# The instructions of a hybrid attention / DeltaNet layer, put in order by a scheduler with a timeline model instead of a plain one

## The chip, the cores and the metric

The kernel runs on one core of a Trainium2 chip. The metric is the device time of one execution in microseconds (us); lower is better. Before the change it is 937.15 us, the median of three runs (936.86 to 937.77).

The engines are named as in the profile: PE is the matrix engine (PEld its weight loads), DVE the vector engine, ACT the scalar engine, POOL the general-purpose engine, SP the engine that only issues transfers here. Each engine takes its instructions strictly in the order in which they stand in its own list. Semaphores tie the lists together.

## The reference

One layer of a diffusion backbone over 512 latent tokens and 256 context tokens, all in float32. The core of it is:

```python
mod = silu(c) @ w_ada + b_ada                       # adaLN, 6 vectors; mod_c the same from c_ctx
h  = rms_norm(x, g_norm1)   * (1 + sc1)  + sh1
hc = rms_norm(ctx, g_norm1) * (1 + csc1) + csh1
aq, ak, av, dq, dk, dv, dz, da, db, ga, gd = split_cols(h @ w_in)   # the same for hc
y_attn = window_ctx_attention(rope(q), rope(k), v, k_ctx, v_ctx, sink)      # 8 heads, 2 KV heads, window 128
_, s_cf, s_cb = bidir_delta(context inputs, zero state)              # gated DeltaNet, chunks of 64, two directions
o_dl, _, _    = bidir_delta(latent inputs, s_cf, s_cb)
y_d = rms_norm(o_dl) * silu(dz)
y = sigmoid(ga) * (y_attn @ w_br_attn) + sigmoid(gd) * (y_d @ w_br_dn)
x = x + gt1 * (y @ w_out)
x = x + gt2 * (square(relu(modulated_norm(x) @ w_mlp1)) @ w_mlp2)
```

The DeltaNet part inverts a unit-triangular 64 x 64 matrix for each chunk and head, and carries a 64 x 64 state per head through 4 context and 8 latent chunks, forwards and backwards.

## The kernel before, in words

Activations lie with channels on the 128 partitions and the 512 (or 256) tokens along the free axis. A float32 product is made of three matmuls on values split into a high and a low part (`mm3`: high x high, high x low, low x high; lines L289, L290, L291; the gate tiles do the same at L943, the attention branch at L988). Each weight tile of 128 x 1024 arrives by `wload`: a transfer by SP into one of four raw buffers, then a copy of the high part by ACT (L240) and a subtraction for the low part by DVE (L241):

```python
raw = sb.tile([P, KT, P], F32, tag="wr", bufs=NWR, name=nm("wr"))[:, :n]     # NWR = 4
nc.sync.dma_start(out=raw, in_=src)
A.activation(r32(hi), raw, AF.Copy)
V.tensor_tensor(r32(lo), raw, hi, op=ALU.subtract)
```

All other buffers in SBUF and PSUM come from an arena at fixed addresses, handed out in program order.

The program runs through these stages. In *startup* the adaLN vectors are made from `w_ada` (L207, L226) and the inputs are normalised and split. The *input projection* follows; meanwhile the DeltaNet's small 32 x 32 and 64 x 64 products are made (half products L699, decay sums L718), and the triangular matrices are inverted on DVE. The *attention* runs over 8 units of query block and KV head. Then come the 4 *context steps* of the DeltaNet's chain, with the branch projection (L988) and gate tiles (L943) woven in. The two *combines* put the inverted halves together: 64 matmuls of 32 x 32 at L793/L794, a copy by ACT, and 64 more at L803/L804, each of them two passes on PE. The 8 *latent steps* of the chain run PE L1055 -> DVE L1059, L1060 -> PE L1067 -> DVE L1073 -> PE L1086 (and L1104 for the output) -> DVE L1097 -> PE L1055 of the next step, for both directions in turn. Between these parts the program text puts gate-tile matmuls as fill (`FILL[3] = (8, 7, 3)` in each step) and one late adaLN column (`late_mod`: one 512 KB transfer into a raw weight buffer and one DVE multiply-and-sum at L1009):

```python
for n, _ in enumerate(steps(range(NCC, NC_))):
    run_fill(FILL[3][n % 3])
    if n % 3:
        run_late(LATE)
```

Then the chain's output is normalised and transposed (L1219, L1224, L1229), the DeltaNet branch and the output projection follow, the second norm (L1297 sums squares over partitions, once for each half of the tokens), and the MLP, some 330 us of `mm3` in a row.

The program text is only a first order. The whole program stands inside one `tile.TileContext`, and its scheduler makes each engine's list: it takes the instructions whose inputs are due by its own model of the time that each takes, and so moves them ahead of or behind one another, within the dependencies. The order around the change is therefore set by that model.

## Time and profile before

| | |
|---|---|
| median of three runs | 937.15 us (936.86 to 937.77) |
| the profiled execution | 938.35 us, its span 936.5 us |
| mean granted clock of PE | 0.991 |
| PE busy | 901.0 us, 96% of the span, 7736 matmuls |
| DVE busy | 596.2 us, 64% |
| ACT busy | 443.0 us, 47% |
| moved by DMA | 98.72 MB, 105 GB/s on average |

PE counts as busy also while its pipeline fills, so a busy PE is not one at its peak. The shares are averages over stages that differ a great deal: DVE is nearly full between 100 and 200 us and idle for more than half of the MLP.

### The profile page before, as it was taken

What the parts mean: (1) busy time and instruction counts of PE and PEld (TensorE: products, weight loads), DVE (VectorE), ACT (ScalarE), POOL (GpSimd) and SP (SyncE); (2) the same over time, 40 slices, a digit from 0 to 9 for tenths busy, and PEclk for the clock granted to TensorE, in tenths of its full rate; (3) what the DMA queues carried; (4) which work ended last, traced back from release to release, by engine and by line L of the source; (5) the groups of instructions that cost most, each with busy time, mean ns of one, the idle gap of its engine ahead of it and who ended that gap; (6) DMA issues with size and microseconds to landing.
All of it is one profiled execution on the core that took longest, in us unless ns stands there. A gap on an engine that the chain in (4) does not pass through costs nothing.

```text
span 936.5 us, 18158 instructions
## 1 busy us (share of the span) xinstructions
PE 901.0 (96%) x7736; PEld 730.0 (78%) x7736; DVE 596.2 (64%) x1013; ACT 443.0 (47%) x815; POOL 12.1 (1%) x26
## 2 busy tenths in 40 slices
PE   7999889999999999989999998999999999999998
PEld 5688667877777677778888888988888888888886
DVE  4666779997877998358875977982454235434411
ACT  5467635338567887475555434660243125213400
POOL 0000000000000001000000000000000000000000
PEclk8999989999999999999999999999999999999999
DMA  9921111210000132225424474481344124222111
GB/s 350 347 69 46 47 47 46 68 46 24 23 11 24 34 114 92 93 92 162 157 86 136 157 273 137 143 291 39 115 152 138 45 68 156 92 67 91 45 43 47
DMA packets 29600, 98.72 MB, mean 105 GB/s; under 512 B 3664, under 2 KB 4176, under 8 KB 29520
## 3 DMA queue, kind: packets, MB, share of 16 engines
q1 hardware_dynamic: 29520, 97.57, 31.5%
q8 instruction: 60, 0.98, 0.4%
q14 instruction: 20, 0.16, 0.1%
HBM read 95.46 MB, written 2.10 MB: 104 GB/s over the span
## 4 chain that ended last, share of the span: by engine, by line
PE 72%; DVE 12%; ACT 8%; DMA 4%; issue 3%; SPq 0%; DVEq 0%; ACTq 0%
PE banks L289 16%; PE banks L290 15%; PE banks L291 15%; PE banks L943 9%; PE banks L988 2%; DMA wr<-in_wm 2%; PE banks L1055 2%; DMA wa<-in_wada 2%; DVE wl L241 1%; ACT m L146 1%; PE banks L1086 1%; PE banks L1067 1%; PE banks L526 1%; DVE m L183 1%; PE banks L207 1%
## 5 line engine op out<-in xcount | busy, mean ns | idle before, releaser
L289 PE MATMUL banks<-m,m 128*128 128x512 f32 (+1 forms) x584 | 219.4, 379 | 3.4 <-ACT m L240 3.0
L290 PE MATMUL banks<-m,m 128*128 128x512 f32 (+1 forms) x584 | 219.0, 377 | 0.1
L291 PE MATMUL banks<-m,m 128*128 128x512 f32 (+1 forms) x584 | 218.9, 377 | 0.0
L240 ACT ACTIVATE m<-wr 128x1024 fp32r<-128x1024 f32 x67 | 70.8, 1058 | 157.9 <-PE banks L290 78.9
L289 PEld LDWEIGHTS banks<-m,m 128*128 128x128 f32 x584 | 109.2, 188 | 26.4 <-ACT m L240 3.1
L241 DVE TENSOR_TENSOR m<-wr,m 128x1024 fp32r<-128x1024 f32 x67 | 81.9, 1224 | 70.3 <-PE banks L290 34.2
L290 PEld LDWEIGHTS banks<-m,m 128*128 128x128 f32 x584 | 109.5, 188 | 21.7 <-DVE m L241 0.8
L291 PEld LDWEIGHTS banks<-m,m 128*128 128x128 f32 x584 | 109.3, 188 | 21.2 <-issue 0.8
L289 PE MATMUL banks<-m,wh 128*128 128x512 f32 (+1 forms) x312 | 114.1, 366 | 0.9 <-DVE m L1270 0.6
L291 PE MATMUL banks<-m,wl 128*128 128x512 f32 (+1 forms) x312 | 111.5, 360 | 2.3 <-DVE wl L241 2.3
L290 PE MATMUL banks<-m,wh 128*128 128x512 f32 (+1 forms) x312 | 111.0, 356 | 0.0
L943 PE MATMUL banks<-m,wh 128*128 128x512 f32 x320 | 103.9, 399 | 0.0
L1371 DVE SCALAR_TENSOR_TENSOR m<-banks,modT,m 128x512 f32<-128x512 f32 x32 | 24.0, 750 | 101.0 <-PE banks L291 101.0
L241 DVE TENSOR_TENSOR wl<-wr,wh 128x1024 fp32r<-128x1024 f32 (+1 forms) x60 | 64.7, 1079 | 28.4 <-ACT wh L240 28.2
L240 ACT ACTIVATE wh<-wr 128x1024 fp32r<-128x1024 f32 (+1 forms) x60 | 56.6, 944 | 31.5 <-PE banks L290 15.0
L943 PEld LDWEIGHTS banks<-m,wh 128*128 128x128 f32 x320 | 59.1, 188 | 12.1
L291 PEld LDWEIGHTS banks<-m,wl 128*128 128x128 f32 x312 | 58.8, 189 | 11.3 <-DVE wl L241 3.0
L289 PEld LDWEIGHTS banks<-m,wh 128*128 128x128 f32 x312 | 59.3, 190 | 10.4 <-DVE m L1270 0.8
L290 PEld LDWEIGHTS banks<-m,wh 128*128 128x128 f32 x312 | 59.3, 190 | 7.5 <-issue 0.2
L943 PE MATMUL banks<-m,wl 128*128 128x512 f32 x160 | 65.0, 406 | 0.0
L182 ACT ACTIVATE m<-m 128x512 fp32r<-128x512 f32 (+1 forms) x56 | 35.2, 631 | 48.9 <-DVE m L1354 21.1
L183 DVE TENSOR_TENSOR m<-m,m 128x512 fp32r<-128x512 f32 (+1 forms) x56 | 38.3, 689 | 18.8 <-ACT m L182 18.3
(231 smaller groups left out, 1274.7 us busy)
## 6 DMA issues: line engine op xcount, KB each, us to landing
wr<-in_wm SPq DMA_DIRECT2D x64, 512.0 KB, 3.5
wr<-in_win SPq DMA_DIRECT2D x39, 512.0 KB, 3.5
wa<-in_wada SPq DMA_DIRECT2D x32, 512.0 KB, 4.0
m<-in_wada SPq DMA_DIRECT2D x16, 512.0 KB, 10.2
m<-in_xT SPq DMA_DIRECT2D x8, 512.0 KB, 6.1
wr<-in_wbr SPq DMA_DIRECT2D x16, 256.0 KB, 2.7
wr<-in_wout SPq DMA_DIRECT2D x8, 512.0 KB, 4.7
out<-m SPq DMA_DIRECT2D x8, 256.0 KB, 2.0
```

What stands on the lines that cost most here:

```text
L146: r = A.activation(out_, in_, func, **kw)
L182: A.activation(r32(hi), src, AF.Copy)
L183: (eng or V).tensor_tensor(r32(lo), src, hi, op=ALU.subtract)
L240: A.activation(r32(hi), raw, AF.Copy)
L241: V.tensor_tensor(r32(lo), raw, hi, op=ALU.subtract)
L289: PE.matmul(acc, w[0][:, k, :], xhi, start=(start and i == 0), stop=False)
L290: PE.matmul(acc, w[0][:, k, :], xlo, start=False, stop=False)
L291: PE.matmul(acc, w[1][:, k, :], xhi, start=False, stop=(stop and i == n - 1))
L943: PE.matmul(acc.ap, w[x][:, k, :], hx[k][y], start=(k == p == 0), stop=(k == KT - 1 and p == 2))
L988: PE.matmul(pa.ap, w[x][:, j, :], r32(Q[y][:, :, j, :]), start=(j == p == 0), stop=(j == 3 and p == 2))
L1055: PE.matmul(z[r, x * 256 + q * HD:x * 256 + (q + 1) * HD], src[q][r, col(c):col(c) + CH], S[r, q * HD:(q + 1) * HD], start=True, stop=True)
L1371: V.scalar_tensor_tensor(xn_[ct], acc.ap, modT[:, 3, ct:ct + 1], xn_[ct], op0=ALU.mult, op1=ALU.add)
```

## The change

```diff
-    with tile.TileContext(nc) as tc:
+    with tile.TileContext(nc, schedule_with_timeline_sim=True) as tc:
         tile_layer(tc, aps, out)
```

The scheduler simulates the engines on a timeline while it picks instructions, where before it used a plain model. Nothing is added or taken away: every engine has the same instructions with the same operands and the same buffers at the same addresses, in another order. POOL's order stays as it was. SP's changes in a few places: in startup the constants and four weight loads go ahead of the last adaLN loads. ACT, DVE and PE change from startup to the branch projections; in the MLP their orders are the same but for a few neighbours. Three places on PE follow; a row gives the line, the operation, the written and the read buffers, the size, and how many stand in a row.

The first is a latent step of the chain, from its L1067 on (`wh` and `wl` are a gate tile's weights, `m_3026` the state). Before:

```order
L1067 MATMUL banks<-m_4772,m_3696 64x64 x8
L1067 MATMUL banks<-m_4791,m_3700 64x64 x8
L943 MATMUL banks<-m_184,wh_4602 128x512
L943 MATMUL banks<-m_184,wl_4603 128x512
L943 MATMUL banks<-m_184,wh_4602 128x512 x2
L943 MATMUL banks<-m_184,wl_4603 128x512
L943 MATMUL banks<-m_184,wh_4602 128x512 x2
L943 MATMUL banks<-m_184,wl_4603 128x512
L1086 MATMUL banks<-m_4820,m_3523 64x64 x8
L1104 MATMUL banks<-m_4822,m_4071 64x64 x8
L1086 MATMUL banks<-m_4837,m_3585 64x64 x8
L1104 MATMUL banks<-m_4839,m_4072 64x64 x8
```

And now:

```order
L1067 MATMUL banks<-m_4772,m_3696 64x64 x8
L1067 MATMUL banks<-m_4791,m_3700 64x64 x8
L1086 MATMUL banks<-m_4820,m_3523 64x64 x8
L1104 MATMUL banks<-m_4822,m_4071 64x64 x8
L1055 MATMUL banks<-m_3026,m_578 64x64 x2
L1055 MATMUL banks<-m_3026,m_579 64x64 x2
L1055 MATMUL banks<-m_3026,m_580 64x64 x2
L1055 MATMUL banks<-m_3026,m_581 64x64 x2
L1055 MATMUL banks<-m_3026,m_2073 64x64
L1086 MATMUL banks<-m_4837,m_3585 64x64 x8
L1104 MATMUL banks<-m_4839,m_4072 64x64 x8
```

Here the eight gate matmuls behind L1067 are gone, and the next step's L1055 of one direction begins before the other direction's L1086. Before, each of the first seven latent steps holds 18 gate matmuls in three or four groups. Now the steps hold, from the first on, 40, 24, 24, 0, 13, 13, 16 and 31 or so: most of the fill stands in the first three, and none from the L1067 of the third step until after the L1055 of the fifth.

The second is the seam between the two halves of the first combine for the latent chunks (`m_774` and `m_775` are the inverted halves of the two groups). Before:

```order
L794 MATMUL banks<-m_3701,m_774 32x32
L943 MATMUL banks<-m_184,wh_3635 128x512
L943 MATMUL banks<-m_184,wl_3636 128x512
L943 MATMUL banks<-m_184,wh_3635 128x512 x2
L943 MATMUL banks<-m_184,wl_3636 128x512
L943 MATMUL banks<-m_184,wh_3635 128x512 x2
L943 MATMUL banks<-m_184,wl_3636 128x512
L943 MATMUL banks<-m_184,wh_3709 128x512 x2
L943 MATMUL banks<-m_184,wl_3710 128x512
L943 MATMUL banks<-m_184,wh_3709 128x512
L803 MATMUL banks<-m_3696,m_3729 32x32
L804 MATMUL banks<-m_3700,m_3729 32x32
```

And now:

```order
L794 MATMUL banks<-m_3701,m_775 32x32
L793 MATMUL banks<-m_3697,m_775 32x32
L794 MATMUL banks<-m_3701,m_775 32x32
L803 MATMUL banks<-m_3696,m_3729 32x32
L804 MATMUL banks<-m_3700,m_3729 32x32
L803 MATMUL banks<-m_3696,m_3729 32x32
```

The 12 gate matmuls between the halves are gone, and part of the second group's products fills their place. Before, small matmuls stood in groups of 64 with 12 to 24 gate matmuls between them. Now 199 stand in one row (7 of L1055, 90 of L793/L794, 64 of L803/L804, 38 of L793/L794).

The third is the second norm (L1297 adds the squares of one half of the tokens; `m_6434` is the first MLP weight). Before:

```order
L1297 MATMUL banks<-m_6012,ones 128x256
L289 MATMUL banks<-m_5824,wh_6226 128x256
L290 MATMUL banks<-m_5824,wh_6226 128x256
L291 MATMUL banks<-m_5824,wl_6227 128x256
L289 MATMUL banks<-m_5825,wh_6226 128x256
```

And now:

```order
L291 MATMUL banks<-m_5828,wl_6227 128x256
L1297 MATMUL banks<-m_6012,ones 128x256 x2
L289 MATMUL banks<-m_6217,m_6434 128x256
L289 MATMUL banks<-m_6217,m_6440 128x256
L289 MATMUL banks<-m_6217,m_6446 128x256
L290 MATMUL banks<-m_6217,m_6434 128x256
```

Before, the first L1297 had 15 matmuls of the output projection behind it and the second stood 64 matmuls later, inside the MLP's first products. Now both stand side by side, behind the whole output projection and ahead of the whole MLP.

## The prediction

> **What bounds the kernel now.** First the page, then stretches of the span by stage, then what PE waits for, then the chain of waits around its longest stops. The page:

> ```profile
> PE 901.0 (96%) x7736; PEld 730.0 (78%) x7736; DVE 596.2 (64%) x1013; ACT 443.0 (47%) x815; POOL 12.1 (1%) x26
> PE 72%; DVE 12%; ACT 8%; DMA 4%; issue 3%; SPq 0%; DVEq 0%; ACTq 0%
> ```

> PE is busy 96% of 936.5 us, and 72% of the chain that ended last is PE's own work. An order that changes no instruction can only win back PE's idle time, 35 us, or add to it. The stretches (length, then the busy time of PE, PEld, DVE, ACT and POOL, granted clock, DMA share, GB/s) say where it lies:

> ```profile
> 0.00:31.00 31.00, 23.41 (x146) 15.48 (x146) 14.51 (x30) 16.23 (x23) 0.21 (x4) 0.83 0.94 365
> 31.00:100.00 69.00, 69.00 (x592) 54.97 (x590) 43.24 (x85) 41.53 (x67) 1.47 (x2) 1.00 0.32 112
> 100.00:200.00 100.00, 90.22 (x1043) 72.21 (x1041) 91.70 (x173) 44.09 (x74) 0.00 (x0) 0.97 0.17 54
> 200.00:300.00 100.00, 94.14 (x762) 72.15 (x763) 79.96 (x155) 67.41 (x138) 2.07 (x4) 1.00 0.07 22
> 360.00:415.00 55.00, 51.59 (x1306) 41.58 (x1304) 29.49 (x37) 30.98 (x53) 8.31 (x16) 1.00 0.31 98
> 415.00:500.00 85.00, 83.89 (x1345) 67.84 (x1341) 61.83 (x132) 49.97 (x157) 0.00 (x0) 1.00 0.37 117
> 605.00:937.00 332.00, 327.55 (x1444) 270.65 (x1442) 136.45 (x157) 93.76 (x116) 0.00 (x0) 1.00 0.31 100
> ```

> Idle PE time is 7.6 us in startup (transfers at 365 GB/s, 94% of the queues), 9.8 us in 100 to 200 us (DVE at 92%: the inversion), 5.9 us in the attention, 3.4 us around the combines and only 1.1 us in the latent steps. The MLP from 605 us keeps its order, so its 332 us stand. The stops by releaser (total, times, longest):

> ```profile
> PE banks L699 <- issue: 5.9, 2, 3.3
> PE banks L289 <- ACT m L240: 3.0, 1, 3.0
> PE banks L485 <- DVE m L575: 1.7, 1, 1.7
> PE banks L526 <- DVE m L543: 1.5, 1, 1.5
> PE banks L276 <- DVE m L273: 1.3, 1, 1.3
> PE banks L793 <- issue: 1.3, 1, 1.3
> ```

> The largest, "issue", is a wait that no semaphore ends. The chain shows where (start, length, what), and the table of queues what runs then:

> ```profile
> 114.02 1.37 PE banks L699 x87
> 115.39 3.34 issue
> 118.72 0.86 PE banks L699 x45
> ...
> 121.16 0.43 PE banks L718
> ...
> 124.84 0.23 PE banks L718
> ...
> 133.05 2.52 issue
> ...
> q8 instruction: 60, 0.98, 0.4%
> ```

> PE's 7736 matmuls and 7736 weight loads are fetched in 60 packets, so one packet of 16 KB holds about 128 matmuls. Where a hundred or so small matmuls stand packed, PE eats a packet's worth in 1 to 2 us and then stops for 2.5 to 3.3 us. I read "issue" there as PE running out of fetched instructions. After the longer stop the same L718 takes 0.43 us a piece instead of 0.23 until 124 us: the clock is at half.

> **The change, part by part.** Nothing is added or removed; the terms are the places where a stall goes, comes or loses its cover. They add to the profiled execution's 938.35 us, which lies 1.2 us over the median, 937.15; since they are differences I add them to the median.

> *Startup, -1.5 us.* In the new order ACT's first weight split does not stand behind as much normalisation, so the waits of 3.0 us (L289 on L240) and 1.3 us (L276 on L273) may shrink: -4.3 us at best. Against it SP issues four weight tiles and the constants ahead of the last adaLN pairs. That is about 2 MB; at 365 GB/s the last pair lands some 5 us later. What hides it is PE's backlog, 69.00 of 69 us from 31 us on; with that cover gone it costs +5. I take a third of the best case.

> *100 to 360 us, 0.* The inversion's DVE work starts earlier, some query work on DVE later, and the sum on DVE is the same. Waits such as L485 on L575 (1.7) and L526 on L543 (1.5) may go and others come. DVE at 91.70 of 100 leaves no room for much gain, and nothing is added to it. L699's half products stand a little more packed, with about as many packets overrun as before. Bounds -6 (two thirds of the 9.8 idle) to +6 (the same again).

> *Combines, +4.5 us.* 199 small matmuls stand in a row where groups of 64 had 12 to 24 gate matmuls between them. Each passes PE twice, so 398 passes with their loads, about 3.1 packets, are to be eaten in

> ```profile
> L794 PE MATMUL banks<-m,m 32*32 32x32 f32 x128 | 2.8, 193 | 0.0
> L793 PE MATMUL banks<-m,m 32*32 32x32 f32 x128 | 2.7, 193 | 1.3 <-issue 1.3
> 368.27 0.21 PE L793 MATMUL banks<-m,m 32*32 32x32 f32 x1
> ...
> 369.48 0.50 PE L943 MATMUL banks<-m,wh 128*128 128x512 f32 x1
> ```

> some 3.4 us: the first burst of 128 passes ran from 368.27 us to the gate matmul at 369.48, some 1.1 to 1.2 us. At 114 us one burst of 192 passes met one stop, so 398 passes should meet two: 2 x (2.52 to 3.34) = 5.0 to 6.7 us. Less the 1.3 us that L793 waits today, 3.7 to 5.4; I take 4.5. Lower bound 0 (the bursts of 128 passes mostly run without a stop today, so packets are fetched ahead), upper 8.7 (three stops of 3.34, less 1.3).

> [...]

> *Latent steps, +5.6 us.* The durations on DVE in 415 to 500 us, and two successive steps on PE:

> ```profile
> L1009 DVE SCALAR_TENSOR_TENSOR m<-wa,m 128x1024 f32<-128x1024 f32 x13 | 15.8, 1219 | 1.2 <-DMA wa<-in_wada 1.1
> L1009 DVE DVE_READ_ACCUMULATOR m<-wa,m 128x1 f32 x13 | 1.1, 81 | 0.0
> L1097 DVE TENSOR_TENSOR m<-m,banks 128x256 f32<-128x256 f32 x14 | 5.9, 418 | 8.0 <-PE banks L1086 6.6 <-ACT m L1079 1.0
> L581 DVE SCALAR_TENSOR_TENSOR m<-m,banks 128x512 f32<-128x512 f32 x4 | 2.7, 682 | 0.0
> 420.58 2.08 PE L1055 MATMUL banks<-m,m 64*64 64x64 f32 x64
> 422.59 0.50 PE L943 MATMUL banks<-m,wl 128*128 128x512 f32 x1
> 422.93 0.63 PE L943 MATMUL banks<-m,wh 128*128 128x512 f32 x2
> 423.40 0.39 PE L943 MATMUL banks<-m,wl 128*128 128x512 f32 x1
> 424.63 1.15 PE L1067 MATMUL banks<-m,m 64*64 64x64 f32 x32
> 430.43 2.08 PE L1055 MATMUL banks<-m,m 64*64 64x64 f32 x64
> ```

> A step takes 430.43 - 420.58 = 9.85 us, and PE is full: 18 gate matmuls at 0.23 (from 422.93 to 423.40 two take 0.47) are 4.1 us, the small ones about 5.1 us (L1055 2.0, L1067 1.1, and L1086 with L1104 2.0), the rest is lost where sizes change (0.34 us from 422.59 to 422.93 instead of 0.23). In the new order PE has no fill between the L1067 of the third step and that of the fourth: 5.1 us of work. DVE has, from L1073 to L1073 there, five late products (5 x 1.30), ten operations of 128x256 (10 x 0.42) and two silu products (2 x 0.68): 12.1 us, or 10.8 with neighbours overlapping by some 0.07 us. They stand between the chain's own operations in DVE's list, so PE waits 10.8 - 5.1 = 5.7 us. The neighbouring steps add about 1 (13 gate matmuls, 3.0 us, cover less of the round trip PE-DVE-PE than 18 did). The fill itself is not lost: 161 gate matmuls stand in the steps instead of 141, all to be done anyway. Fewer changes of size, 20 groups of fill instead of 25, give back 5 x 0.22 = 1.1 us. 5.7 + 1 - 1.1 = +5.6. Bounds -1.1 (DVE gets ahead) to +12, where late products also wait for their transfer (this view: 1.1 us at L1009 today).

> *Branch projection, +0.5 us.* 13 gate matmuls (3.0 us) instead of 51 (11.5 us) stand between the transposes L1224 and the first product that needs DVE's result; the first result is some 2 us away. 0 to +4.

> *Second norm, +2 us.* Rows of ACT and DVE after the first L1297, which starts at 579.2 us:

> ```profile
> 579.89 0.47 ACT L146 ACTIVATE m<-banks,epsc 128x256 f32<-128x256 f32 x1 [0.67 <-PE banks L1297]
> 580.40 0.42 ACT L146 ACTIVATE m<-m 128x256 f32<-128x256 f32 x1
> 580.85 1.27 DVE L294 SCALAR_TENSOR_TENSOR m<-m,mA,m 128x256 f32<-128x256 f32 x3 [1.17 <-ACT m L146]
> 581.37 1.31 ACT L295 ACTIVATE m<-m,modT 128x256 fp32r<-128x256 f32 x3 [0.55 <-DVE m L294]
> ```

> The first normalised tile is there at 581.8 us, 2.6 us after L1297 began. Now 15 matmuls cover it (0.12 us each for 256 columns, 1.8 us). In the new order nothing stands between, and PE in its turn waits at the second L1297 for the last residual. +2 us; 0 to +4.

> Sum: -1.5 + 0 + 4.5 + 5.6 + 0.5 + 2 = +11.1 us, so 937.15 + 11.1 = 948.2 us.

> **The rivals.**

> *Faster: the stalls go and no new ones come.* If packets are fetched ahead and DVE runs its late products while PE does the fill that now stands in front, the two large terms are 0. If besides the waits that the earlier DVE and ACT work can lift (3.0 + 1.7 + 1.5 + 1.3 = 7.5 us in the list above) all go: 929.7 us. For it: these waits have DVE or ACT as releaser, and both have idle time before 100 us (DVE 43 of 69). Against: the chain's operations follow each other by data, so DVE cannot be ahead of them. It decides once combines and steps together lose less than these waits give back beyond the norm and the branch projection: under 7.5 - 2.5 = 5 us.

> *No change.* Terms of both signs cancel: 937 us. For it: the work is the same to the last instruction, and PE stays 96% busy. Against: the saturated steps can only lose.

> *Slower still: the clock falls.* Where a stop in the combines or the third step goes on for 3 us or more, the matmuls behind it run at 0.43 instead of 0.23 for some 4.6 us, as up to 124 us: about 2 us for each stop. With three such, and two late products each waiting 2 us for a transfer: +10 us more, 958 us. For it: the stop of 3.34 us did so. Against: that of 2.52 us did not.

> [...]

> **How the numbers follow.** Forecast 0.49, clock 0.14, no change 0.14, faster 0.23. A measurement here tells 0.2%, about 1.9 us, from nothing. Slower by more: 0.49 + 0.14 = 0.63; same 0.14; faster 0.23. The likeliest case alone, with its bounds taken half way, spans 941 to 956 us. Eight in ten over all cases need 931 (most of the faster case) to 958 us.

> **What would show it.** Right: a row "issue" of 2 us or more at L793 or L803, PE idle on DVE L1073 or L1059 with L1009 ahead of it in the third and fourth latent step, a step of some 11 us there, PE idle 2 us at L1297 or the L289 behind it, and the MLP of the same length. Wrong: the small matmuls of the combines run through, or the steps' total from the first L1055 to the last L1104 grows by no more than the 20 added gate matmuls (4.6 us). The forecast falls if PE's idle time before 360 us changes by more than 6 us either way.

## The result, and the profile after

The changed kernel takes 994.3 us (median of four runs, 991.79 to 997.77) where the kernel before, run beside it, takes 937.46 us (936.86 to 939.39). The ratio is 1.0601, with a 95% interval of 1.0578 to 1.0624: 56 us slower, where 11 were forecast and 958 us was the upper end of the range. The profiled execution took 993.18 us, its span 991.4, at a mean granted clock of 0.957 (0.991 before).

The page of the changed kernel first: busy time by engine, and the granted clock of PE in 40 slices, in tenths.

```profile
PE 926.0 (93%) x7736; PEld 753.5 (76%) x7736; DVE 597.2 (60%) x1013; ACT 443.4 (45%) x815; POOL 12.0 (1%) x26
PEclk8999989989999899889699999999999999999999
```

DVE, ACT and POOL do what they did, to within 1 us. PE has the same 7736 matmuls, yet 25 us more busy time: the clock is slower in places (half clock makes 8.9 us by the measure below), and what makes the rest was not measured. The dip of the clock to 6 in the twentieth slice lies in the latent steps. Next the stretches (length, busy time of PE, PEld, DVE, ACT, POOL, granted clock, DMA share, GB/s), cut at the same two events in each kernel. The attention goes from the first to the last L549, the latent steps from their first L1067 to the last L1104. Before:

```profile
206.80:300.10 93.30, 87.64 (x732) 67.33 (x730) 73.76 (x141) 63.73 (x129) 2.07 (x4) 1.00 0.06 18
414.00:488.40 74.40, 73.37 (x1315) 59.44 (x1315) 55.09 (x123) 45.44 (x151) 0.00 (x0) 1.00 0.40 129
```

And after, with 21 us out of the middle of the steps as a third row:

```profile
204.00:312.80 108.80, 96.68 (x742) 75.00 (x743) 73.76 (x141) 63.98 (x130) 2.07 (x4) 0.94 0.06 18
443.20:539.20 96.00, 82.41 (x1323) 68.09 (x1322) 56.27 (x124) 42.09 (x141) 0.00 (x0) 0.89 0.33 100
474.00:495.00 21.00, 14.34 (x256) 13.64 (x256) 14.43 (x32) 7.06 (x25) 0.00 (x0) 0.59 0.56 176
```

Between the same events lies nearly the same work: 10 matmuls more in the attention, where DVE's work is the same to the last instruction (73.76 us), and 8 more in the steps. But the attention takes 15.5 us more and the steps 21.6. In the third row PE is idle a third of the time and its granted clock is 0.59.

For the whole program I measured each matmul's time to the next one against the usual time for its line and width in the kernel before (the lower quartile). The excess is called a stop where it is over 0.3 us, half clock where a shorter one exceeds 60% of that usual time in a matmul 128 or more columns wide, and rest otherwise (22 to 30% of it stands next to a change of size). What is left is work, and it is 786.5 us in both kernels, which have the same matmuls. The excess by stage:

| from ... to | before, us | after, us | more |
|---|---|---|---|
| start, first L699 | 26.8 | 28.4 | 1.6 |
| first scores L485 | 24.6 | 21.5 | -3.1 |
| first L549 | 3.3 | 2.3 | -1.0 |
| last L549 (attention) | 16.3 | 29.4 | 13.1 |
| first L988 (branch projection) | 1.4 | 7.3 | 5.9 |
| last L988 (context steps) | 8.7 | 6.6 | -2.1 |
| second combine's L794 | 4.5 | 6.0 | 1.5 |
| last L804 (combine) | 6.4 | 12.7 | 6.3 |
| first latent L1067 | 9.1 | 13.3 | 4.2 |
| last L1104 (latent steps) | 36.4 | 56.3 | 19.9 |
| first L1224 | 0.5 | 0.3 | -0.2 |
| first L1297 | 3.7 | 8.4 | 4.7 |
| last L291 (end of the MLP) | 3.1 | 7.4 | 4.3 |

Each row runs from the event of the row above to its own. The rows add to 55.1 us, the difference of the two spans to within 0.3. One execution stands behind each column, and executions of one kernel lie up to 7 us apart (935.19 to 941.96 us in the first run below), so a row of 2 or 3 us says little. By kind, stops go from 49.0 to 90.9 us (+41.9), half clock from 18.1 to 27.0 (+8.9), the rest from 77.9 to 82.1 (+4.2). So three quarters of the loss is PE standing still. What it waits for after (us in total, times, longest):

```profile
PE banks L1067 <- DVE m L1060: 6.2, 4, 3.4
PE banks L699 <- issue: 5.2, 4, 2.2
PE banks L803 <- ACT m L795: 5.1, 2, 3.4
PE banks L1086 <- ACT m L1077: 4.6, 2, 3.7
PE banks L526 <- ACT m L146: 3.6, 3, 1.9
PE banks L291 <- DVE wl L241: 3.3, 3, 2.4
PE banks L1055 <- issue: 3.1, 1, 3.1
PE banks L533 <- DVE m L183: 3.1, 5, 1.5
...
PE banks L793 <- issue: 2.5, 1, 2.5
PE banks L290 <- DVE m L296: 2.0, 1, 2.0
...
PE banks L1297 <- DVE m L1274: 1.3, 1, 1.3
```

The list is longer and flatter than before, when "issue" at L699 was its head with 5.9 us. The rows "issue" grew little: those of L699, L1055 and L793 are 10.8 us together, and 8.1 before. Most of the new rows are round trips: PE gives a result to ACT or DVE and waits for the answer. The attention (L526, L533) and the chain's steps (L1067, L1086, L1055) have most of them.

### The profile page after: what moved, and what is told of

The parts are those of the page before. It is cut to its first block, busy times and chain, and to the rows that moved or that the text cites. A ratio compares the mean times of both kernels' runs of the same rounds, so it can differ in the third digit from the quotient of the medians.

```text
span 991.4 us, 18185 instructions
## 1 busy us (share of the span) xinstructions
PE 926.0 (93%) x7736; PEld 753.5 (76%) x7736; DVE 597.2 (60%) x1013; ACT 443.4 (45%) x815; POOL 12.0 (1%) x26
## 4 chain that ended last, share of the span: by engine, by line
PE 71%; DVE 15%; ACT 6%; DMA 4%; issue 3%; DVEq 0%; ACTq 0%
PE banks L289 15%; PE banks L290 15%; PE banks L291 15%; PE banks L943 10%; DMA wa<-in_wada 3%; DVE wl L241 2%; PE banks L988 2%; ACT m L146 2%; DVE m L183 1%; PE banks L1067 1%; PE banks L591 1%; PE banks L188 1%; PE banks L526 1%; PE banks L1055 1%; DVE m L773 1%
## 5 line engine op out<-in xcount | busy, mean ns | idle before, releaser
L290 PE MATMUL banks<-m,m 128*128 128x512 f32 (+1 forms) x584 | 220.3, 379 | 2.0 <-DVE m L296 2.0
L291 PE MATMUL banks<-m,m 128*128 128x512 f32 (+1 forms) x584 | 219.3, 378 | 0.0
L289 PE MATMUL banks<-m,m 128*128 128x512 f32 (+1 forms) x584 | 216.9, 380 | 0.9 <-ACT m L295 0.9
L240 ACT ACTIVATE m<-wr 128x1024 fp32r<-128x1024 f32 x67 | 70.7, 1058 | 162.1 <-PE banks L290 80.2
L290 PEld LDWEIGHTS banks<-m,m 128*128 128x128 f32 x584 | 110.8, 190 | 23.1 <-DVE m L296 2.2
L289 PEld LDWEIGHTS banks<-m,m 128*128 128x128 f32 x584 | 109.7, 190 | 24.3 <-ACT m L295 3.9
L291 PEld LDWEIGHTS banks<-m,m 128*128 128x128 f32 x584 | 110.9, 190 | 20.6 <-DVE modA L229 0.4
L241 DVE TENSOR_TENSOR m<-wr,m 128x1024 fp32r<-128x1024 f32 x67 | 81.8, 1224 | 70.3 <-PE banks L290 34.2
L289 PE MATMUL banks<-m,wh 128*128 128x512 f32 (+1 forms) x312 | 113.9, 367 | 1.9 <-ACT wh L240 0.7
L291 PE MATMUL banks<-m,wl 128*128 128x512 f32 (+1 forms) x312 | 111.5, 359 | 3.3 <-DVE wl L241 3.3
L290 PE MATMUL banks<-m,wh 128*128 128x512 f32 (+1 forms) x312 | 112.2, 360 | 0.0
L943 PE MATMUL banks<-m,wh 128*128 128x512 f32 x320 | 107.1, 411 | 0.0
L241 DVE TENSOR_TENSOR wl<-wr,wh 128x1024 fp32r<-128x1024 f32 (+1 forms) x60 | 64.5, 1077 | 35.3 <-ACT wh L240 35.2
L240 ACT ACTIVATE wh<-wr 128x1024 fp32r<-128x1024 f32 (+1 forms) x60 | 56.4, 942 | 52.6 <-PE banks L290 32.0
L943 PEld LDWEIGHTS banks<-m,wh 128*128 128x128 f32 x320 | 61.5, 195 | 13.5 <-DVE m L543 0.2
L291 PEld LDWEIGHTS banks<-m,wl 128*128 128x128 f32 x312 | 59.9, 192 | 13.0 <-DVE wl L241 4.4
L289 PEld LDWEIGHTS banks<-m,wh 128*128 128x128 f32 x312 | 60.1, 193 | 12.3 <-ACT wh L240 1.6
L290 PEld LDWEIGHTS banks<-m,wh 128*128 128x128 f32 x312 | 60.0, 192 | 8.5 <-issue 0.7
L943 PE MATMUL banks<-m,wl 128*128 128x512 f32 x160 | 65.6, 410 | 0.0
L182 ACT ACTIVATE m<-m 128x512 fp32r<-128x512 f32 (+1 forms) x56 | 35.2, 630 | 47.1 <-DVE m L1354 21.0
L1009 DVE SCALAR_TENSOR_TENSOR m<-wa,m 128x1024 f32<-128x1024 f32 x32 | 38.9, 1221 | 22.2 <-DMA wa<-in_wada 21.8
```

The lines of the kernel that those rows point to most:

```text
L182: A.activation(r32(hi), src, AF.Copy)
L289: PE.matmul(acc, w[0][:, k, :], xhi, start=(start and i == 0), stop=False)
L290: PE.matmul(acc, w[0][:, k, :], xlo, start=False, stop=False)
L291: PE.matmul(acc, w[1][:, k, :], xhi, start=False, stop=(stop and i == n - 1))
L943: PE.matmul(acc.ap, w[x][:, k, :], hx[k][y], start=(k == p == 0), stop=(k == KT - 1 and p == 2))
L1009: V.scalar_tensor_tensor(t.ap, wa, 0.5, scr.ap, op0=ALU.mult, op1=ALU.mult, accum_out=modT[:, grp, j:j + 1])
```

## The experiments

The question was where the 56 us are made, and by what. To put one part of the new order into the old program, a table of instruction numbers is added, and each engine's instructions are tied into its sequence. The tie is an order of issue only and adds no wait. No run has the old order in this table alone; that the first run below comes out at 1.0003 leaves little room for a cost of the tie itself.

```diff
     with tile.TileContext(nc) as tc:
         tile_layer(tc, aps, out)
+        pin_order(tc, nc)
+def pin_order(tc, nc):
+    nosync = mybir.DependencyInfo(mybir.DependencyClass.NoSync, mybir.DependencyReason.DATA)
+    ins = {i.name: i for i in nc.cur_bb.bb.instructions}
+    last = {}
+    for n in ORDER:
+        i = ins["I-" + n]
+        if i.engine in last:
+            tc.add_manual_dep(i, last[i.engine], nosync, reason="pinned order")
+        last[i.engine] = i.name
```

Below, a diff of `ORDER` stands for the table, written short: `old[a:b]` is a stretch of the old order of all 7782 instructions, and `by_new(...)` is the same stretch sorted as the new order has it. Every kernel here does all of the computation. Ratios are against the kernel before run on the same chip, with their 95% intervals; a loss in us is the ratio's excess times 937.46 us.

**One stage at a time.** Theory A says that each stage's loss is made by that stage's own order, so that single stages lose what the whole loses there and the losses add. The rival is that losses are handed on from stage to stage, through the clock or through a delay on DVE or in the transfers. Five runs cover the program: startup and inversion, attention, context steps with combines, latent steps, and all that comes behind the chain.

```diff
-ORDER = old
+ORDER = by_new(old[:1471]) + old[1471:]                        # e1_start
+ORDER = old[:1471] + by_new(old[1471:2723]) + old[2723:]       # e2_attn
+ORDER = old[:2723] + by_new(old[2723:4046]) + old[4046:]       # e3_ctx_comb
+ORDER = old[:4046] + by_new(old[4046:5161]) + old[5161:]       # e4_steps
+ORDER = old[:5161] + by_new(old[5161:])                        # e5_tail
```

> All engines keep the old order except in the first stretch (startup, input projection, inversion, up to the first attention scores), which stands in the new order. In the two traces the first scores start 1.6 us earlier and the first transposed attention output 2.9 us earlier in the new kernel. Theory A (each stage's loss comes from its own order): 934 to 936 us, 1 to 3 us faster than before. Rival B (the losses are knock-on effects of how an earlier stage leaves buffers, transfers and clock): the new first stretch must make later stages slower, so 940 us or more.

Measured: 1.0003 (0.9982 to 1.0023), 938.18 us, between the two expected ranges. No gain. In the profile of this run the wait of L289 on ACT's L240 (3.0 us) is gone, as forecast, but a new one stands in its place:

```profile
PE banks L207 <- DVE m L269: 3.1, 1, 3.1
```

> Only the attention stage (from the first scores to the first context transposes of the chain) stands in the new order. Between the same marks the new kernel lost some 14 us there. Theory A: 948 to 953 us. Rival B: less than 942 us.

Measured: 1.0191 (1.0161 to 1.0222), 955.88 us: 17.9 us from a stretch to which the forecast gave nothing, and above what was expected here.

> Only the context steps, the combines and the half products before the latent steps stand in the new order. Between the same marks the new kernel lost 15 to 20 us there, of which some 3 us are fill that it merely did earlier. Theory A: 950 to 955 us. Rival B: less than 944 us.

Measured: 1.0104 (1.0056 to 1.0152), 945.77 us, 9.7 us: under the range of theory A, by 4 us.

> Only the latent steps of the chain stand in the new order. Between the same marks the new kernel lost 21 to 25 us there. Theory A: 957 to 962 us. My own forecast for this stretch alone was +5.6 us, 943 us. Rival B: under 948 us, because without the late start the transfers of the late products are there in time.

Measured: 1.0285 (1.0242 to 1.0329), 964.83 us: 26.7 us, the largest share, and above the expected range.

> Only the stretch behind the chain (transposes, branch and output projection, second norm, MLP) stands in the new order. u1_undo left 16.4 us where e3_ctx_comb had 9.8, so Theory A puts some 6.6 us here: 942 to 946 us. My forecast for this stretch was +2.5 us, 939.7 us.

Measured: 1.0101 (1.0060 to 1.0143), 947.94 us, 9.5 us, above what was expected.

What follows: alone, the five stages lose 0.3, 17.9, 9.7, 26.7 and 9.5 us, together 64.1, where the whole change loses 56.3. The table above, grouped in the same way, has -2.5, 19.0 (attention and the row behind it), 9.9, 19.9 and 8.8. (The numbers in the expectations were cut out of the two traces some 11 us ahead of the events named, which put a part of the attention's loss into the stage behind it; the table has the cuts at the events.) So the losses are local, as theory A has it, and three of the five come out alone as they do in the whole. The traces of the two largest show the growth in its place: with the same measure, that of e2_attn grows by 14.2 us from the first to the last L549 and by 5.2 in the row behind it, that of e4_steps by 24.6 in the steps, and no other row of either by more than some 2 us. Only the steps lose more alone, by 7 us (3 to 11 by the interval of that run). Transfers may be a part of that: with the steps alone in the new order, DVE's late products wait longer than in the changed kernel (8.2 us there), and why is open.

```profile
DVE m L1009 <- DMA wa<-in_wada: 12.5, 5, 4.8
```

**Undoing the two largest.** The new order everywhere, but the attention and the latent steps as before.

```diff
-ORDER = new
+ORDER = by_new(old[:1471]) + old[1471:2723] + by_new(old[2723:4046]) + old[4046:5161] + by_new(old[5161:])
```

> The new order everywhere, but the attention and the latent steps stand in the old order. If the losses of the stages add up (Theory A), what is left is that of the context steps and combines (9.8 us in e3_ctx_comb) and some 2 us of the stretches not run alone: 946 to 951 us. If instead the old order of these two stages cannot mend what the new one of the others leaves behind, 960 us or more.

Measured: 1.0175 (1.0155 to 1.0196), 954.88 us, between the two expected ranges: 40 of the 56 us are gone, 16.4 are left. That is more than the 9.7 us that the context steps and combines lose alone. The run of the tail accounts for it: 9.7 + 9.5 + 0.3 = 19.5 us, a little over what is left.

**The attention: where the fill stands.** In the attention PE alternates with ACT (exponentials and copies) and DVE (sums and scalings): scores L485 to L497, transposes L526, products L532 and L533. The fill is the query and gate tiles' `mm3` (L289, L290, L291, and L943 for some gate tiles). Before, it stands in between; a few rows of PE's timeline in the old kernel:

```profile
203.27 0.39 PE L289 MATMUL banks<-m,wh 128*128 128x512 f32 x1
...
204.46 0.49 PE L532 MATMUL banks<-m,m 128*128 128x512 f32 x1
...
204.83 0.48 PE L290 MATMUL banks<-m,wh 128*128 128x512 f32 x1
...
205.38 0.39 PE L289 MATMUL banks<-m,wh 128*128 128x512 f32 x1
```

And the same stage in the changed kernel:

```profile
254.73 0.49 PE L532 MATMUL banks<-m,m 128*128 128x512 f32 x1 [0.69 <-ACT m L182]
...
257.90 0.50 PE L532 MATMUL banks<-m,m 128*128 128x512 f32 x1 [0.69 <-ACT m L182]
...
261.13 0.44 PE L490 MATMUL banks<-m,m 128*128 128x384 f32 x1 [0.76 <-ACT m L146]
...
265.82 1.12 PE L526 MATMUL banks<-c_ident,m 128*128 128x128 f32 x4 [1.93 <-ACT m L146]
...
268.32 0.78 PE L289 MATMUL banks<-m,wh 128*128 128x512 f32 x1
```

From 240.57 to 268.32 us not one fill matmul starts on PE, and the round trips lie bare, those shown with 0.69, 0.69, 0.76 and 1.93 us. Then 17 stand in one row. The three longest such gaps of the changed kernel's attention are 27.7, 18.7 and 15.4 us; the longest before is 6.4 us. To see whether this alone is enough, the next run keeps the old order of ACT, DVE and SP and moves on PE only: the 24 matmuls of each of six such tiles are placed in one row behind the tile's first.

```diff
 L290 MATMUL banks<-m_184,wh_1970 128x512
 L291 MATMUL banks<-m_184,wl_1971 128x512
+L289 MATMUL banks<-m_184,wh_1970 128x512
+L290 MATMUL banks<-m_184,wh_1970 128x512
+L291 MATMUL banks<-m_184,wl_1971 128x512
...
 L526 MATMUL banks<-c_ident,m_1983 128x128 x2
...
-L289 MATMUL banks<-m_184,wh_1970 128x512
-L290 MATMUL banks<-m_184,wh_1970 128x512
-L291 MATMUL banks<-m_184,wl_1971 128x512
```

> Old order on every engine, but in the attention the 24 matmuls of each query or gate tile (six tiles) stand together behind the tile's first one, instead of one to six at a time between the attention's transposes and products. DVE, ACT and SP keep the old order. Theory P (bunched fill leaves PE's round trips over ACT and DVE bare, 17.9 us in e2_attn): 948 to 956 us. Rival (the loss in e2_attn comes from the order on ACT and DVE): less than 942 us.

Measured: 1.0200 (1.0169 to 1.0230), 955.44 us: 18.7 us, the size that the attention lost in the new order (17.9). Its waits from 190 to 355 us:

```profile
PE banks L532 <- ACT m L182: 3.9, 7, 1.3
PE banks L826 <- DVE m L581: 3.6, 2, 2.3
...
PE banks L526 <- ACT m L146: 1.9, 3, 1.5
```

The same lines stop on the same releasers in the changed kernel (between 204 and 327 us there: L526 on L146 3.6, L532 on L182 2.0, L826 on L581 2.0 us), though not in the same shares. Between the first and the last L549 the excess is 30.7 us here and 29.4 in the changed kernel, against 16.3 before. The longest gaps between fill matmuls are 22.7, 21.3 and 16.1 us here. What follows: bunched fill is enough for a loss of this size, without a change on any other engine.

**The latent steps: fill on PE, or late products on DVE.** The forecast saw both, and named DVE's late products as the price. P is the theory that the fill's new places on PE cost the time, D that the late products (L1009) and their transfers do. Two runs separate them: the steps in the new order with the late products and their transfers beside their old neighbours, and the old order with nothing but the gate matmuls of the latent steps (L943) at their new places (40, 24, 24, 0, 13, 13, 16 and 31 in the eight steps, instead of 18 in each of the first seven).

```diff
-ORDER = old
+ORDER = old[:4046] + with_late_as_in_old(by_new(old[4046:5161])) + old[5161:]   # f1_steps_late_old
+ORDER = old[:4046] + with_L943_as_in_new(old[4046:5161]) + old[5161:]           # f2_steps_fill_new
```

> Latent steps in the new order as in e4_steps, but the late products (the multiply-and-sum L1009 on DVE and its transfers) stand behind the same neighbours as in the old order. Theory P (the loss of the steps comes from PE's fill being used up in the first three steps): still 954 to 962 us. Theory D (it comes from late products crowded between the chain's operations on DVE and waiting there for their transfers): 941 to 946 us, what is left being the fill's place.

> Old order on every engine, but the gate matmuls L943 of the latent steps stand behind the same neighbours on PE as in the new order (40, 24, 24, 0, 13, 13, 16, 31 per step). The late products stay where they were. Theory P: 952 to 962 us. Theory D: 940 to 946 us.

Measured: f1 1.0175 (1.0140 to 1.0211), 952.82 us, between its two ranges; f2 1.0178 (1.0132 to 1.0223), 953.49 us, in the range of P. The steps' new order alone lost 26.7. Without its late products it loses 16.4, and nothing else differs between these two runs, so the late products cost 10.3, give or take 5 by the two intervals. The fill's places alone lose 16.7. P and D both hold, P probably with the larger share. That 16.7 and 10.3 add up to 27.0 is partly luck: in f2 ACT and DVE still split the weights in the old order, so fill that was moved forward finds its weights late. PE's waits there have this row, and 0.8 us more for the low part of the weights:

```profile
PE banks L943 <- ACT wh L240: 3.2, 1, 3.2
```

The changed kernel has no wait at L943, so some 4 of the 16.7 us are not its own. The waits of PE from 395 to 520 us, first with the whole new order of the steps, then with the late products put back:

```profile
PE banks L1067 <- DVE m L1060: 9.8, 4, 7.0
PE banks L1055 <- DVE m L1097: 5.1, 4, 3.9
PE banks L1086 <- ACT m L1077: 3.8, 2, 3.0
```

```profile
PE banks L1067 <- DVE m L1060: 6.3, 3, 3.9
PE banks L1055 <- DVE m L1097: 2.1, 3, 1.2
...
PE banks L1086 <- ACT m L1077: 1.2, 2, 0.8
```

All three shrink and none goes away; what is left is, as I read it, round trips without cover. DVE itself waits for the late transfers, and all that stands behind it waits too. DVE's wait over the steps, before and in the changed kernel:

```profile
DVE m L1009 <- DMA wa<-in_wada: 1.1, 2, 0.9
```

```profile
DVE m L1009 <- DMA wa<-in_wada: 8.2, 4, 3.5
```

DVE's timeline in the changed kernel shows what that does in the third and fourth step, and PE's what comes of it (the figure in brackets is the idle time before the row):

```profile
472.79 1.23 DVE L1009 SCALAR_TENSOR_TENSOR m<-wa,m 128x1024 f32<-128x1024 f32 x1 [3.47 <-DMA wa<-in_wada]
...
473.94 0.42 DVE L1073 TENSOR_TENSOR m<-banks,eg 128x256 f32<-128x256 f32 x1
...
494.00 1.23 DVE L1009 SCALAR_TENSOR_TENSOR m<-wa,m 128x1024 f32<-128x1024 f32 x1 [3.10 <-DMA wa<-in_wada]
...
495.15 0.41 DVE L1097 TENSOR_TENSOR m<-m,banks 128x256 f32<-128x256 f32 x1
```

```profile
474.83 1.12 PE L1086 MATMUL banks<-m,m 64*64 64x64 f32 x16 [3.71 <-ACT m L1077]
...
484.93 1.12 PE L1067 MATMUL banks<-m,m 64*64 64x64 f32 x16 [3.38 <-DVE m L1060]
...
495.62 1.15 PE L1055 MATMUL banks<-m,m 64*64 64x64 f32 x32 [1.78 <-DVE m L1097]
```

L1073 at 473.94 belongs to the chain; it stands behind a product whose 512 KB have not landed. Its own operand comes from the L1067 that starts at 469.97 us, so it could have started at about 470.7 (estimated from the L1067 at 497.82, which L1073 follows 0.73 us later). So it is 3.2 us late: 2.1 of the 3.47 us of waiting and the product itself. PE's 3.71 us at L1086 are this delay, passed on through ACT, and the round trip. Where the products are hardly late (0.70 us at 479.97), as ahead of 484.93, PE waits 3.38 us for DVE all the same: two late products (from 479.97 and 482.98 us) and two silu products (L581) stand among DVE's operations of the chain, with no fill on PE to cover them.

The other way round, the late products of the latent steps go back to their old neighbours in the changed kernel. The rows are DVE's.

```diff
 L1073 TENSOR_TENSOR m_4530<-banks,eg 128x256
-L1009 SCALAR_TENSOR_TENSOR m_4754,modT<-wa_4752,m_3691 128x1024
 L1097 TENSOR_TENSOR m_3026<-m_4558,banks 128x256
...
 L1059 TENSOR_TENSOR m_4628<-banks,eg 128x256
+L1009 SCALAR_TENSOR_TENSOR m_4754,modT<-wa_4752,m_3691 128x1024
 L1060 SCALAR_TENSOR_TENSOR m_4628<-m_3346,m_4628 128x256
```

> The new order on all engines, only the late products of the latent steps (L1009 and their transfers) stand behind their old neighbours. In the old kernel this part of the new steps cost 26.7 - 16.4 = 10.3 us. If it costs the same inside the new kernel: 981 to 987 us. If the other stages' new order has its own share in the late transfers: 988 us or more.

Measured: 1.0504 (1.0461 to 1.0548), 986.13 us: 9.1 us less than the change, beside the 10.3 found from the other end, each to within some 5 us. The expectation held.

**Can the old order's own stops be removed?** Two runs on the old order, both on PE alone. In the first, the longest packed rows of L699 (96 and 64 of them, where the two stops marked "issue" lie) get one projection matmul behind every eighth or sixth.

```diff
 L699 MATMUL banks<-m_578 32x32 x8
+L289 MATMUL banks<-m_184,wh_959 128x512
 L699 MATMUL banks<-m_579 32x32 x4
 L699 MATMUL banks<-m_580 32x32 x4
+L290 MATMUL banks<-m_184,wh_959 128x512
```

> Old order, but in the two packed rows of half products (96 and 64 matmuls of L699 at 114 and 133 us) one matmul of the input projection that followed stands behind every 8th or 6th. Theory F (the stops named issue, 3.34 and 2.52 us, and the half clock after the first, some 2 us, are PE waiting for fetched instructions): the projection's matmuls run inside the stops, 931 to 935 us. Rival (the stops have another cause, or DVE sets the pace of this stretch anyway): 936 to 940 us.

Measured: 1.0036 (1.0020 to 1.0051), 940.22 us, slower instead of faster. What PE waits for from 90 to 200 us:

```profile
PE banks L699 <- DVE m L731: 3.1, 2, 1.7
```

No "issue" is left where there were 5.9 us of it, so packed small matmuls are indeed what made it. But PE now waits for DVE, whose inversion fills this stretch (91.70 of 100 us). From the first L699 to the first scores it takes 74.8 us instead of 73.1. The removed stop was slack of PE, not time of the program.

In the second, five or six fill matmuls are pulled ahead of each of four stops of the attention and the context steps (at 200.2, 254.5, 280.3 and 314.8 us); one of the four:

```diff
 L493 MATMUL banks<-m_557,m_553 128x256
+L289 MATMUL banks<-m_184,wh_2447 128x512
+L290 MATMUL banks<-m_184,wh_2447 128x512
+L291 MATMUL banks<-m_184,wl_2448 128x512
...
 L526 MATMUL banks<-c_ident,m_2463 128x128 x2
...
-L289 MATMUL banks<-m_184,wh_2447 128x512
-L290 MATMUL banks<-m_184,wh_2447 128x512
-L291 MATMUL banks<-m_184,wl_2448 128x512
```

> Old order, but at four stops of PE (200.2, 254.5, 280.3 and 314.8 us; 1.8, 1.7, 1.3 and 1.3 us long) five or six projection, gate or branch matmuls that stood 0.3 to 1.5 us later stand ahead of the waiting instruction. Theory P says that fill ahead of a wait is worth what it covers: up to 5.9 us less, 932 to 935 us. Rival (as in s1_spread: ACT or DVE set the pace there, the stop only moves): 936.5 to 939 us.

Measured: 1.0023 (1.0009 to 1.0038), 940.32 us, again slightly slower. Its waits from 190 to 310 us:

```profile
PE banks L289 <- DVE m L550: 3.0, 1, 3.0
PE banks L526 <- ACT m L146: 2.3, 3, 1.1
PE banks L943 <- DVE m L543: 1.3, 1, 1.3
```

The covered stops are gone or smaller (L485 on L575 was 1.7 us, L532 on L182 was 1.3), and others have come behind them: the attention's excess goes from 16.3 to 20.4 us. At two of the four stops, those at 254.5 and 280.3 us, the fill that was pulled ahead waits for DVE itself: L289 stops for 3.0 us on L550 where the old order stopped for 1.5, and L943 for 1.3 on L543 where it stopped for 1.1. I read this as the bank that the fill writes not being free yet; which bank that is, no trace shows. And behind the first of them, fill that was spent is missing: L526 at 260.02 us waits 1.05 us for ACT, where the old order had no stop. So this run does not show what free fill ahead of a stop is worth.

No order that was run beats the old one. No run has the new order of DVE and ACT with the old one of PE, so what those two engines' order costs by itself is open. Why the scheduler's timeline model bunches the fill stays open too; no trace shows that model.

## Why the prediction was wrong

**The sign was right, the size was not**: +56 us instead of +11.1. Term by term, with what the single-stage runs and the table of the excess give:

*Startup, -1.5 forecast.* Measured +0.3 for startup and inversion together (0.9982 to 1.0023); the table has -2.5, from one execution of each. The wait of L289 on L240 went, as the step said. A wait of its size is new, L207 for DVE's L269 with 3.1 us; the step asked only what SP's transfers would cost and not what the moved ACT and DVE work would be late for.

*100 to 360 us, 0 forecast. This step failed first.* "The sum on DVE is the same", it said, and the bounds of 6 us were taken from idle time. The sums are the same, and the attention alone lost 17.9 us. A sum of busy time says how much fill there is, not whether some of it stands in each round trip. The text on the change noted bunching only in the steps, and the same question was not asked of the attention's fill; the run that only bunches it lost 18.7 us.

*Combines, +4.5.* Two fetch stops were forecast for the row of 199. One came, at L793. The chain of waits of the changed kernel has it and another, 32 us later, at the L1055 behind the packed half products (L699), a row that the term did not count:

```profile
399.25 2.46 issue
...
431.27 3.13 issue
```

At L793 that is 2.46 us instead of 1.3: +1.2, so the row's term was three to four times too large. With the other, which was 0.9 us before, it is +3.4, and that this comes near 4.5 is luck. What had no term is L803, which waits 5.1 us for ACT (0.5 before), 3.4 of them in one stop ahead of the first of these rows. ACT's timeline shows why:

```profile
391.89 2.58 ACT L813 ACTIVATE m<-m 32x512 f32<-32x512 f32 x4 [6.39 <-DVE m L783]
394.49 1.06 ACT L240 ACTIVATE wh<-wr 128x1024 fp32r<-128x1024 f32 x1
...
395.93 0.59 ACT L795 ACTIVATE m<-banks 128x512 f32<-128x512 f32 x1
```

The copy L795 that PE waits for stands behind 4.0 us of other ACT work (391.89 to 395.93), released late by DVE's L783. The 12 gate matmuls that were taken from this seam are 2.8 us; by their length they could cover most of the stop, though no run puts back these twelve alone. The forecast counted them as separators of small matmuls and not as the cover of this copy. From the second combine's L794 to the first latent L1067 the excess grew by 10.5 us.

*Latent steps, +5.6.* 26.7 us alone, 19.9 in the table. The mechanism was seen (late products ahead of the chain's operations on DVE, no fill on PE), and the sum was made for one step. Three things in it were too small. "The fill itself is not lost" holds for its work, but not for its cover, and the fill's places alone lost 16.7 us, some 4 of them for weights that came late in that run alone. "The neighbouring steps add about 1" had the wrong size: the starts of the steps' L1067 from 443.24 us on lie 12.7, 14.1, 15.0, 12.9, 9.4 and 11.3 us apart where 9.85 was the pitch before, so the third and fourth steps are long but not alone. And the late transfers, put at the upper bound, came: DVE's wait went from 1.1 to 8.2 us, and the late products with their transfers cost 9.1 to 10.3.

*Branch projection and second norm, +0.5 and +2.* Alone, all that is behind the chain lost 9.5 us (8.8 in the table, none of it before L1224). L1297 waits 1.3 us and L290 behind it 2.0: that is 3.3 beside the 2 forecast, and the mechanism was right. Beside it stand weight tiles whose low part is late (L291 on L241: 3.3 us, 1.5 before) in the projections, where the term had looked only at L1224, and two stretches of 3.41 us at a granted clock of 0.50, from 596.95 and 637.91 us. When this stage alone has the new order, DVE's late products wait 5.2 us there for transfers:

```profile
DVE m L1009 <- DMA wa<-in_wada: 5.2, 5, 3.0
```

*The rivals.* The faster case fell: of the waits that it counted on, L289's went and one of its size came at L207. The slower one, by the clock and late transfers, had the right ingredients: half clock grew by 8.9 us where it allowed 6 (the stretch it took for 4.6 us of half clock is 5.3, from 118.72 to 124.00 us, at a granted clock of 0.50), and DVE's wait for transfers by 7.1 in the steps where it allowed 4. But it was priced on top of 11 us, and stops alone grew by 41.9. *The signs given* read as follows: "issue" of 2 us or more at L793 came (2.5), PE idle with L1009 ahead came, L1297 came; the step is some 13 to 15 us, not 11. The MLP did not change: 341 us at its end hold 337.56 us of PE after and 336.55 before. The condition by which the forecast was to fall, PE's idle time before 360 us changing by more than 6 us, was narrowly not met: it is 24.6 us before and 30.1 after. Counted to the same event, the first L988, it grew by 6.6. The excess up to there grew by 16.5 us in the table: much of what PE loses counts as busy time, half clock for one.

The step of the working that failed is thus a single one, made twice: fill was treated as an amount. The terms for the attention (0) and for the steps (5.6) both keep the amount and lose the places (the steps' late transfers, put at a bound only, come on top), and these two stages made 44.6 of the 64.1 us that the stages lose alone.

## What to carry to other kernels

What independent matmuls are worth on a unit that alternates with others depends on where they stand: count the round trips of a stage and ask of each what covers it, since equal sums of busy time before and after say nothing (here 0 forecast and 18 us lost). Work that waits for a transfer must not stand between a serial chain's operations on the same engine, as its delay is passed on to the whole chain (L1073 was held back by some 3.2 us, and PE then stood for 3.71). And the removal of stops on an engine that did not set the pace was worth nothing (5.9 us of fetch stops gone, and the program 0.4% slower). Fill pulled ahead of a stop has to be able to run there itself (pulled ahead, L289 stopped for 3.0 us where the old order stopped for 1.5).

## What the runs showed of the hardware

The clock fell on less than the prediction assumed. It had one stop of 3.34 us with half clock (granted 0.50 from 117.17 to 124.00 us) and one of 2.52 us without (1.00 behind it). In the changed kernel the clock fell behind a stop of 1.93 us at L526. The granted clock is the figure behind the five busy times:

```profile
257.90:265.80 7.90, 4.96 (x28) 3.48 (x28) 5.42 (x11) 5.26 (x13) 0.00 (x0) 1.00 0.00 0
265.80:268.30 2.50, 2.48 (x12) 2.17 (x13) 1.29 (x4) 0.69 (x2) 0.00 (x0) 0.51 0.00 0
```

Ahead of it PE was busy 4.96 of 7.90 us, with several shorter stops. Four transposes took 0.60 us before and 1.12 behind the stop, and full clock is back at 269.27 us. So in these two executions the length of a single stop does not tell where the clock fell.

What the small matmuls are packed with mattered too: the rows of L699 that stopped for 5.9 us in all ran without such a stop when a wide matmul stood behind every sixth or eighth. In each of the four stops named here (from 115.39 and 133.05 us before, from 399.25 and 431.27 after) one 16 KB packet of the instruction queue starts, at 116.40, 133.22, 399.28 and 432.14 us, which fits the prediction's reading of them as waits for instructions.
